# Late tokens of a PEER mixer: indices kept on chip, unwanted rows skipped, the gather ending two units later

## The chip, the cores and the metric

The kernel runs on one core of a Trainium2 chip. The metric is the device time of one execution in microseconds (us). The kernel before the change took 1620.73 us, the median of three timed runs (1619.91 to 1622.59). One more execution was recorded by the hardware profiler; every time below that is not one of those three comes from it.

Engines are called by the names of the profile: PE (matrix multiply; PEld its weight loads), DVE (vector), ACT (activations), POOL (issues the gathers here), SP (issues most plain transfers). Each engine works through its own instructions strictly in order, so an instruction that waits holds up all that stand behind it on the same engine.

## The reference

The input is 512 tokens of width 1024. One layer runs a hybrid mixer (16 state-space heads and 8 attention heads), a layer norm, a PEER expert mixer, and a last layer norm. The change lies in the PEER part, of which the reference reads, cut down:

```python
q = (xb @ w_query).reshape(T, 8, 2, 128)
s = einsum('thkd,hknd->thkn', q, sub_keys)          # 2 x 128 sub-key scores per head
sv, si = top_k(s, 16)                               # best 16 of each half
cand_s = sv[:, :, 0, :, None] + sv[:, :, 1, None, :]
cand_i = si[:, :, 0, :, None] * 128 + si[:, :, 1, None, :]
top_s, top_pos = top_k(cand_s, 16)                  # 16 experts of 16384, per head
expert_idx = take_along_axis(cand_i, top_pos)
gate = softmax(top_s)
u = u_table[expert_idx]                             # 16384 x 1024
act = gelu(einsum('td,thkd->thk', xb, u))
v = v_table[expert_idx]
out = einsum('thk,thkd->td', gate * act, v)
```

So each token picks 8 x 16 = 128 experts. Expert number 128 i + j lies in chunk i of the tables, a chunk being 128 rows.

## The kernel before

**Two ways of doing PEER.** For the first three blocks of 128 tokens the kernel does not gather. It multiplies the tokens with whole chunks: a U chunk (`u_chunk`, 128 rows of the U table against the tokens, then a gelu into `act`), later a V chunk (`v_chunk`, which weighs `act` with a matrix of gates `gt` and multiplies with 128 rows of the V table into the accumulators `va`). There are 128 chunks of each. For the fourth block of tokens the rows are gathered one expert slot at a time: an indirect transfer issued by POOL brings 128 rows of 4 KB, one per token, into a tile `row`, and DVE takes a dot product with the token (U half, line 1830) or adds the row, weighed, to `ac` (V half, line 1850).

**The 32 late tokens.** Of the third block, 32 tokens (`UG`) get their U dots by an early gather. Another 32 tokens, the late ones (`LT`), take part in U chunks 0 to 51 like the rest (`C1` = `LEAD` = 52), but not in chunks 52 to 127, whose products are therefore 320 columns wide and no longer 352. What they need there is gathered late: `late_fetch` (line 1789) issues 32 indirect transfers of 128 rows (32 tokens times 4 experts each), `late_dots` (line 1795) takes 32 dot products on DVE (line 1802), and `late_build` makes gate matrices of them. `late_build` uses only experts in chunks 52 and up, though the rows of all experts are gathered.

**Where the late indices come from.** `ug_index` (line 1192) works out the expert numbers early. SP writes those of the late tokens to a scratch tensor `lgi` in DRAM. At the start of the gather section, some 220 us later, POOL loads them back in the order needed, as tile `lix` (line 1751), and after that loads `lg` and the small identity `lid`.

**How each stage is fed.** Every chunk of U, V and other weights goes through one stream (`Stream`, lines 84 to 138): SP loads a raw chunk of 512 KB into one of three buffers `wir`, ACT rounds it into `wih` or `wihx` (line 114), DVE subtracts to get the remainder `wil` (line 124), and PE multiplies with both parts. A raw buffer is loaded again once DVE has made its remainder.

**Interleaving.** The order of instructions on each engine is written out by the program. The last loop makes one U chunk and one V chunk per turn while U chunks remain, then one V chunk per turn. In each turn it also draws work from the generator `gather()` through `pump`, which emits steps until their estimated cost is used up. Until the 256 row steps of the fourth block begin, that is 4.0 us of estimated cost per turn. From there on the pace is set by:

```python
units = lambda: (128 - uc) * 2 + WV * (uc - vc)
left = units()
want = 271 - max(0.0, 274 * (left - ENDU) / GS[1])   # GS[1] = units() - ENDU at the first row
while more and GS[0] < want:
    more = pump(fill, 0.1)
```

So the rows are to be done when `ENDU` units are left, a unit being half of a U-and-V turn, or, after the last U chunk, 1/0.86 of a V chunk. The pace is fixed at 66 U chunks and 14 V chunks done, when 62 x 2 + 0.86 x 52 = 168.72 units are left.

**Memory at the start of the gather section.** The pool `gs1` holds the staging tile `stg` whose last store to DRAM, `gsp<-stg` (1920 KB, issued by ACT), is still running when the section begins. The pool `gp2` is opened in the place of closed pools. In the built program `stg` lies at bytes 169216 to 185599 of each partition; the tile `x3` with the late tokens (shown as x) begins at 171392 and the first row buffer at 176000, so both must wait for that store. `x3` is loaded by one transfer that reads 32 token rows four times over (outermost size 4, step 0).

Of the kernel before, what the change touches and what calls it, by code (L numbers as in the profile page):

```python
# [11 lines left out]
F32 = mybir.dt.float32  # L12
# [3 lines left out]
I32 = mybir.dt.int32  # L16
U32 = mybir.dt.uint32
AF = mybir.ActivationFunctionType
OP = mybir.AluOpType
# [17 lines left out]
LT = 32  # L37
C1 = LEAD
# [3 lines left out]
ROWS = 5  # L42
STAIRS = ((0, 0, 1, 16), (16, 1, 3, 8), (40, 4, 12, 4))
DOT0, HEAD0 = 1, 36
ENDU = 15
WV = 0.86
GST = (1, 3, 5, 7)
YST = (18, 19, 20, 21, 22, 24, 25, 26)
# [10 lines left out]
def tile_block(ctx: ExitStack, tc: tile.TileContext, I, out):  # L59
    nc = tc.nc  # L60
    ctx.enter_context(tc.manual_schedule())
    V, A, T, G = nc.vector, nc.scalar, nc.tensor, nc.gpsimd
# [18 lines left out]
    def chain(*gs):  # L81
        for g in gs:
            yield from g
# [128 lines left out]
    lgi = dram.tile([LT, 128], I32, name="lgi")  # L212
    lgg, lgh = (dram.tile([LT, 128], F32, name=n) for n in ("lgg", "lgh"))
# [624 lines left out]
    def v_proj(p):  # L838
        wh, wl = item()
        vh = ml.tile([128, NB, 256], F32R, name="vh", bufs=2)  # L840
        vl = ml.tile([128, NB, 256], F32R, name="vl", bufs=2)
        vv[p] = (vh, vl)
        for b2 in range(2):
            ps = pp()
            for e in range(2):
                b = b2 * 2 + e
                bs = slice(b * 128, (b + 1) * 128)
                for k in range(2):
                    ks = slice(k * 256, k * 256 + 256)
                    mm3(ps[:, e * 256:(e + 1) * 256], kvh[:, k, bs], kvl[:, k, bs], wh[:, ks], wl[:, ks],  # L850
                        k == 0, k == 1)
            evac(ps, vh[:, b2 * 2:b2 * 2 + 2].rearrange("p a b -> p (a b)"),
                 vl[:, b2 * 2:b2 * 2 + 2].rearrange("p a b -> p (a b)"))
            yield

    def qk_nope(h):
        wh, wl = item()
        ps = pp()
        for k in range(3):
            ks = slice(k * 128, k * 128 + 128)  # L860
            mm3(ps, wh[:, ks], wl[:, ks], qlh[:, k], qll[:, k], k == 0, k == 2)
        QN[h] = pair("qn")
        A.activation(QN[h][0], ps, AF.Copy, scale=SCALE)
        if h:
            V.scalar_tensor_tensor(QN[h][1], ps, SCALE, QN[h][0], op0=OP.mult, op1=OP.subtract)
        yield
        if h == 0:
            V.scalar_tensor_tensor(QN[h][1], ps, SCALE, QN[h][0], op0=OP.mult, op1=OP.subtract)
        ps = pp()
        for k in range(2):  # L870
            ks = slice(384 + k * 128, 512 + k * 128)
            mm3(ps, wh[:, ks], wl[:, ks], kvh[:, k], kvl[:, k], k == 0, k == 1)
        KN[h] = pair("kn")
        evac(ps, *KN[h])
        yield
# [69 lines left out]
    g = chain(qk_nope(1), v_proj(0))  # L945
# [4 lines left out]
    for st in range(39):  # L950
        h, q = divmod(st, 4)
        if q == 0 and h:
            g = iter(())
            if h < 7:
                g = chain(qk_nope(h + 1), v_proj(h // 2)) if h % 2 == 0 else chain(q_pe(h // 2 + 1), qk_nope(h + 1))
# [234 lines left out]
    GT, UR = {}, {}  # L1190

    def ug_index():
        ijg = IJG[2]
        f = lambda z: z.rearrange("p h k -> p (h k)")
        ix = rt2.tile([128, 128], I32, name="uii")
        V.scalar_tensor_tensor(ix, f(ijg[:, 0]), 128.0, f(ijg[:, 1]), op0=OP.mult, op1=OP.add)
        G.dma_start(ugi, ix[128 - UG:])
        G.dma_start(ugg, f(ijg[128 - UG:, 2]))
        late = slice(128 - UG - LT, 128 - UG)
        nc.sync.dma_start(lgi, ix[late])  # L1200
        nc.sync.dma_start(lgg, f(ijg[late, 2]))
        G.dma_start(UR["ix"], bass.AP(tensor=ugi.tensor, offset=ugi.offset, ap=[[UG, 128 // UG], [128, UG], [1, UG]]))
        G.dma_start(UR["g"], ugg)
        for n in range(3):
            ug_fetch(n)

    def ug_fetch(n):
        if n < UG:
            UR[n] = ug.tile([128, D], F32, name="urow", bufs=3)
            G.indirect_dma_start(out=UR[n], out_offset=None, in_=I["u"],  # L1210
                                 in_offset=bass.IndirectOffsetOnAxis(ap=UR["ix"][:, n:n + 1], axis=0))
# [241 lines left out]
    ijp = pool("ijp", side="right")  # L1453
# [51 lines left out]
    for m in range(17):  # L1505
# [8 lines left out]
        while tm[1] < tm[0] + T_Q:  # L1514
            c = next(fill, None)
            if c is None:
# [7 lines left out]
    G.dma_start(UR["x"], bass.AP(tensor=xsp.tensor, offset=xsp.offset + (3 * 128 - UG) * D,  # L1524
                                       ap=[[0, 128 // UG], [D, UG], [1, D]]))
    UR["ix"] = ijp.tile([128, UG], I32, name="uix")
    UR["g"] = ijp.tile([UG, 128], F32, name="ugw")
    rt2 = pool("rt2")
    lo_on[0] = V
# [112 lines left out]
    LR, LS = {}, [None]  # L1642
# [84 lines left out]
    def gather():  # L1727
        ix = gp_.tile([128, 128], I32, name="ix")
# [5 lines left out]
        LR["gT"] = gp_.tile([128, LT // 2, 2, 2], F16, name="lgT")  # L1734
        l0 = 128 - UG - LT
        jT, _, dT = GT[2]
        A.activation(LR["io"], iotaE, AF.Copy)
        A.activation(LR["d"], dT[:, :, l0:l0 + LT], AF.Copy)
        A.activation(LR["j"], jT[:, l0:l0 + LT], AF.Copy)
# [4 lines left out]
                                ap=[[0, 128 // LT], [D, LT], [1, D]]))  # L1744
        hd = gp2.tile([128, 128], F32, name="hd")
        R = {}
        r3 = pool("r3", side="right")
        IA["t"] = r3.tile([128, 16, 16], F16, name="ia3")
        nc.sync.dma_start(IA["t"].rearrange("p a b -> p (a b)"), I["ch"][:, 256:512])
        lix = r3.tile([128, LT], I32, name="lix")  # L1750
        G.dma_start(lix, bass.AP(tensor=lgi.tensor, offset=lgi.offset, ap=[[LT, 128 // LT], [128, LT], [1, LT]]))
        LR["g"] = r3.tile([LT, 128], F32, name="lg")
        G.dma_start(LR["g"], lgg)
        LR["w"] = r3.tile([LT, 128], F32, name="lw")
        LR["m"] = r3.tile([LT, 2], F32, name="lm")
        LR["id"] = r3.tile([LT, LT], F32, name="lid")
        G.dma_start(LR["id"], I["idn"][:LT, :LT])
        lhd = r3.tile([128, LT], F32, name="lhd")

        def part(h0):  # L1760
# [28 lines left out]
        def late_fetch(n):  # L1789
            if n < LT:  # L1790
                R[n] = gp2.tile([128, D], F32, name="row", bufs=ROWS)
                G.indirect_dma_start(out=R[n], out_offset=None, in_=I["u"],
                                     in_offset=bass.IndirectOffsetOnAxis(ap=lix[:, n:n + 1], axis=0))

        def late_dots():
            for n in range(ROWS - 1):
                late_fetch(n)
            yield 6.0
            for n in range(LT):
                late_fetch(n + ROWS - 1)  # L1800
                r = R.pop(n)
                V.scalar_tensor_tensor(r, r, 1.0, lx, op0=OP.mult, op1=OP.mult, accum_out=lhd[:, n:n + 1])
                yield 1.2
            A.activation(lhd, lhd, AF.Gelu)
            G.dma_start(bass.AP(tensor=lgh.tensor, offset=lgh.offset, ap=[[LT, 128 // LT], [128, LT], [1, LT]]), lhd)
            G.dma_start(LR["w"], lgh)
            LS[0] = late_build()
# [55 lines left out]
    gp_ = pool("gp")  # L1863
# [7 lines left out]
    while vc <= LASTC:  # L1871
# [15 lines left out]
        else:  # L1887
            left = units()
            want = 271 - max(0.0, 274 * (left - ENDU) / GS[1])
            while more and GS[0] < want:  # L1890
                more = pump(fill, 0.1)
            if more and left < ENDU:
                more = pump(fill, 1.2)
# [8 lines left out]
        if GS[0] >= 0 and GS[1] == 0:  # L1902
            GS[1] = units() - ENDU
    held = {}
# [141 lines left out]
```

## Time and profile before

| | |
|---|---|
| median of three timed runs | 1620.73 us |
| profiled execution, its own time | 1615.43 us |
| span of its instructions | 1613.7 us |
| PE busy / DVE busy | 1550.5 us (96%) / 1372.7 us (85%) |
| ACT busy / POOL busy | 682.8 us (42%) / 594.8 us (37%) |
| bytes moved | 421.63 MB, mean 261 GB/s |
| start of the gather section, first late row, first row of the fourth block | about 756, 776.8 and 867.5 us |
| last row of the fourth block added | 1537.3 us |

A row of the timeline gives the start, the duration, engine, line, operation, output and inputs, and in brackets how long the engine had been idle and what ended that. A row of the windows gives, for a stretch of time, the busy time of PE, PEld, DVE, ACT and POOL (with instruction counts), the granted TensorE clock as a share of full speed, the mean busy share of the 16 DMA engines and the rate. A row of the waits gives who waited for whom: total, times, longest.

### The profile page before, as it was taken

How to read it: one execution, taken by the hardware profiler on the slowest of the kernel's cores; microseconds unless marked ns; L12 is line 12 of the kernel's file. 1: busy time of each engine (PE TensorE's matmuls, PEld its weight loads, DVE VectorE, ACT ScalarE, POOL GpSimd, SP SyncE). 2: the span in 40 equal slices, each digit the busy share in tenths (PEclk: the TensorE clock that was granted, in tenths of full speed). 3: DMA queues.
4: the chain of work that ended last, by engine and by line, in shares of the span. 5: the costliest groups of instructions: out<-in, count | busy, mean ns of one | idle time of the engine just before them, and what ended most of it. 6: DMA issues, size and time to landing. Idle time of an engine off the chain costs nothing.

```text
span 1613.7 us, 23969 instructions
## 1 busy us (share of the span) xinstructions
PE 1550.5 (96%) x8726; PEld 1360.9 (84%) x8726; DVE 1372.7 (85%) x2594; ACT 682.8 (42%) x1060; POOL 594.8 (37%) x426
## 2 busy tenths in 40 slices
PE   8999999999999999999699999989999989899998
PEld 6888788888889999999689899888888878788886
DVE  8988678747798999995598998988889888999977
ACT  5574466632334455554234343233333333333332
POOL 0000031300343133300462555665666656666500
PEclk9999999999999999999899999999999999999999
DMA  6242133472433599997898999999999999999972
GB/s 249 93 169 79 50 82 85 147 243 95 123 112 103 183 301 350 351 285 231 297 382 286 320 335 331 339 335 409 354 363 388 379 367 354 385 377 376 376 258 107
DMA packets 163350, 421.63 MB, mean 261 GB/s; under 512 B 14928, under 2 KB 68096, under 8 KB 162976
## 3 DMA queue, kind: packets, MB, share of 16 engines
q1 hardware_dynamic: 61024, 212.37, 37.7%
q0 software_dynamic: 50928, 181.65, 30.4%
q10 hardware_dynamic: 51280, 26.09, 5.4%
q8 instruction: 68, 1.11, 0.3%
q14 instruction: 50, 0.41, 0.1%
HBM read 385.70 MB, written 32.24 MB: 259 GB/s over the span
## 4 chain that ended last, share of the span: by engine, by line
PE 60%; issue 12%; DVE 11%; DMA 9%; POOL 7%; ACT 1%; DVEq 0%; POOLq 0%; SPq 0%; ACTq 0%
POOL row L1819 6%; PE va L1633 6%; PE va L1630 6%; PE va L1629 5%; PE pu L77 5%; PE pu L79 5%; PE pu L78 5%; DMA row<-v,ix 4%; PE pw L77 3%; PE pw L78 3%; PE pw L79 3%; DVE wil L124 3%; PE pa L77 3%; PE pa L79 3%; PE pa L78 3%
## 5 line engine op out<-in xcount | busy, mean ns | idle before, releaser
L114 ACT ACTIVATE wih<-wir 128x1024 fp32r<-128x1024 f32 (+2 forms) x268 | 277.2, 1035 | 389.2 <-DMA wir<-v 163.0
L79 PE MATMUL pu<-XTH,wil 128*128 128x320 f32 (+1 forms) x1000 | 319.4, 319 | 32.6 <-DVE wil L124 32.4
L124 DVE TENSOR_TENSOR wil<-wir,wih 128x1024 fp32r<-128x1024 f32 x236 | 287.6, 1219 | 61.8 <-ACT wih L114 43.9
L77 PE MATMUL pu<-XTH,wih 128*128 128x320 f32 (+1 forms) x896 | 286.7, 320 | 7.7 <-DVE stg L1711 7.3
L1630 PE MATMUL va<-wil,Ph 128*128 128x512 f32 x726 | 284.5, 392 | 0.2 <-DVE wil L124 0.2
L78 PE MATMUL pu<-XTL,wih 128*128 128x320 f32 (+1 forms) x896 | 282.9, 316 | 0.0
L1819 POOL DMA_INDIRECT row<-u,ix x128 | 197.0, 1539 | 139.4 <-DVE row L1830 103.5
L1819 POOL DMA_INDIRECT row<-v,ix x128 | 199.1, 1555 | 115.8 <-DVE ac L1850 92.0
L79 PEld LDWEIGHTS pu<-XTH,wil 128*128 128x128 f32 x1000 | 189.9, 190 | 39.1 <-DVE wil L124 39.0
L77 PEld LDWEIGHTS pu<-XTH,wih 128*128 128x128 f32 x896 | 170.3, 190 | 11.5 <-issue 7.2
L1850 DVE SCALAR_TENSOR_TENSOR ac<-row,hd,ac 128x1024 f32<-128x1024 f32 x128 | 164.2, 1283 | 16.5 <-DMA row<-v,ix 14.3
L1830 DVE SCALAR_TENSOR_TENSOR row<-row,x 128x1024 f32<-128x1024 f32 x128 | 151.8, 1222 | 25.0 <-DMA row<-u,ix 24.9
L78 PEld LDWEIGHTS pu<-XTL,wih 128*128 128x128 f32 x896 | 170.4, 190 | 2.5
L1629 PE MATMUL va<-wih,Ph 128*128 128x512 f32 x432 | 169.4, 392 | 2.9 <-ACT Ph L1604 2.9
L1630 PEld LDWEIGHTS va<-wil,Ph 128*128 128x128 f32 x726 | 136.8, 188 | 26.9 <-DVE wil L124 0.6
L124 POOL TENSOR_TENSOR wil<-wir,wih 128x1024 fp32r<-128x1024 f32 (+3 forms) x32 | 62.7, 1964 | 245.2 <-PE pw L79 114.0
L114 ACT ACTIVATE wihx<-wir 128x1024 fp32r<-128x1024 f32 x67 | 71.0, 1060 | 176.4 <-DMA wir<-v 151.2
L1633 PE MATMUL va<-wih,Pl 128*128 128x512 f32 x432 | 134.5, 393 | 1.1 <-DVE Pl L1612 1.1
L1629 PE MATMUL va<-wihx,Ph 128*128 128x512 f32 x294 | 114.6, 390 | 0.0
L1633 PEld LDWEIGHTS va<-wih,Pl 128*128 128x128 f32 x432 | 81.7, 190 | 19.1 <-DVE Pl L1612 1.9
L1629 PEld LDWEIGHTS va<-wih,Ph 128*128 128x128 f32 x432 | 81.7, 189 | 19.1 <-ACT Ph L1604 3.3
L1633 PE MATMUL va<-wihx,Pl 128*128 128x512 f32 x294 | 90.7, 390 | 0.0
(549 smaller groups left out, 3089.8 us busy)
## 6 DMA issues: line engine op xcount, KB each, us to landing
wir<-ut SPq DMA_DIRECT2D x128, 512.0 KB, 6.5
wir<-v SPq DMA_DIRECT2D x128, 512.0 KB, 6.5
gt<-gsp SPq DMA_DIRECT2D x30, 768.0 KB, 8.8
gsp<-stg ACTq DMA_DIRECT2D x11, 1920.0 KB, 15.4
wir<-wo SPq DMA_DIRECT2D x25, 512.0 KB, 3.7
wir<-wf SPq DMA_DIRECT2D x18, 512.0 KB, 3.7
wir<-wqr SPq DMA_DIRECT2D x16, 512.0 KB, 3.7
de<-acd POOLq DMA_DIRECT2D x8, 512.0 KB, 4.9
```

Source lines behind the costliest of these rows:

```text
L77: T.matmul(ps, lh, rh, start=start, stop=False)
L78: T.matmul(ps, lh, rl, start=False, stop=False)
L79: T.matmul(ps, ll, rh, start=False, stop=stop)
L114: A.activation(h, r, AF.Copy)
L124: self.lo(n).tensor_tensor(l, r, h, op=OP.subtract)
L1629: T.matmul(va[b][e], Ph[b], h[:, cs], start=c == 0, stop=False)
L1630: T.matmul(va[b][e], Ph[b], l[:, cs], start=False, stop=False)
L1633: T.matmul(va[b][e], Pl[b], h[:, cs], start=False, stop=c == (LASTC if b == 2 and e else 127))
L1819: G.indirect_dma_start(out=R[s], out_offset=None, in_=I["u"] if s < 128 else I["v"], in_offset=bass.IndirectOffsetOnAxis(ap=ix[:, s % 128: ...
L1830: V.scalar_tensor_tensor(r, r, 1.0, x3, op0=OP.mult, op1=OP.mult, accum_out=hd[:, s:s + 1])
L1850: V.scalar_tensor_tensor(ac, r, hd[:, s - 128:s - 127], ac, op0=OP.mult, op1=OP.add)
```

## The change

Four things are done.

1. In `ug_index`, DVE makes a second set of indices: to the number of every expert in chunks 0 to 51 it adds 32768, which is past the end of the table. SP stores these to `lgi` and, right behind, loads them back in the order needed into a tile `uli` on chip. At the start of the gather section DVE copies `uli` to `lix`; POOL's load of `lix` is gone.
2. The 32 late indirect transfers get a bound (16383) with which an index beyond it is passed over, so that its row is not brought. The five row buffers are first cleared by DVE, five memsets of 128 x 1024, so that a place whose row is passed over holds a number.
3. POOL's loads of `lg` and `lid` move from ahead of the first late transfers to behind the first four.
4. `ENDU` goes from 15 to 13.

```diff
-ENDU = 15
+ENDU = 13
...
         late = slice(128 - UG - LT, 128 - UG)
-        nc.sync.dma_start(lgi, ix[late])
+        lx_, far = (rt2.tile([128, 128], dt, name=n) for n, dt in (("uil", I32), ("uif", F32)))
+        V.tensor_scalar(far, f(ijg[:, 0]), float(C1), 32768.0, op0=OP.is_lt, op1=OP.mult)
+        V.tensor_tensor(lx_, ix, far, op=OP.add)
+        nc.sync.dma_start(lgi, lx_[late])
         nc.sync.dma_start(lgg, f(ijg[late, 2]))
+        nc.sync.dma_start(UR["li"], bass.AP(tensor=lgi.tensor, offset=lgi.offset, ap=[[LT, 128 // LT], [128, LT], [1, LT]]))
...
     UR["ix"] = ijp.tile([128, UG], I32, name="uix")
+    UR["li"] = ijp.tile([128, LT], I32, name="uli")
...
         jT, _, dT = GT[2]
+        lix = gp_.tile([128, LT], I32, name="lix")
+        V.tensor_copy(lix, UR["li"])
...
-        lix = r3.tile([128, LT], I32, name="lix")
-        G.dma_start(lix, bass.AP(tensor=lgi.tensor, offset=lgi.offset, ap=[[LT, 128 // LT], [128, LT], [1, LT]]))
         LR["g"] = r3.tile([LT, 128], F32, name="lg")
-        G.dma_start(LR["g"], lgg)
         LR["w"] = r3.tile([LT, 128], F32, name="lw")
         LR["m"] = r3.tile([LT, 2], F32, name="lm")
         LR["id"] = r3.tile([LT, LT], F32, name="lid")
-        G.dma_start(LR["id"], I["idn"][:LT, :LT])
...
         def late_fetch(n):
             if n < LT:
                 R[n] = gp2.tile([128, D], F32, name="row", bufs=ROWS)
+                if n < ROWS:
+                    V.memset(R[n], 0.0)
                 G.indirect_dma_start(out=R[n], out_offset=None, in_=I["u"],
-                                     in_offset=bass.IndirectOffsetOnAxis(ap=lix[:, n:n + 1], axis=0))
+                                     in_offset=bass.IndirectOffsetOnAxis(ap=lix[:, n:n + 1], axis=0),
+                                     bounds_check=128 * 128 - 1, oob_is_err=False)
 
         def late_dots():
             for n in range(ROWS - 1):
                 late_fetch(n)
+            G.dma_start(LR["g"], lgg)
+            G.dma_start(LR["id"], I["idn"][:LT, :LT])
             yield 6.0
```

The order on the engines moves at three places. New lines shift the line numbers: 1802 of before is 1810 now, 1612 is 1617, 1586 is 1591, 1792 is 1797, 1850 is 1858, 1856 is 1864.

On DVE at the start of the gather section, before (`wil` is a chunk's remainder, `Pl` and `gt` belong to the gate matrices, `row` is a late dot):

```order
L124 TENSOR_TENSOR wil<-wir,wihx 128x1024
L124 TENSOR_TENSOR wil<-wir,wih 128x1024
L1612 TENSOR_TENSOR Pl<-gt,Ph 128x12x2x32
L124 TENSOR_TENSOR wil<-wir,wih 128x1024
L1802 SCALAR_TENSOR_TENSOR row,lhd<-row,x_8438 128x1024 x2
L124 TENSOR_TENSOR wil<-wir,wih 128x1024
L1586 TENSOR_TENSOR gt<-act,gt 128x11x64
```

and now:

```order
L124 TENSOR_TENSOR wil<-wir,wihx 128x1024
L1743 COPY lix<-uli 128x32
L1796 MEMSET row 128x1024 x4
L124 TENSOR_TENSOR wil<-wir,wih 128x1024
L1617 TENSOR_TENSOR Pl<-gt,Ph 128x12x2x32
L124 TENSOR_TENSOR wil<-wir,wih 128x1024
L1796 MEMSET row 128x1024
L1810 SCALAR_TENSOR_TENSOR row,lhd<-row,x_8446 128x1024 x2
L124 TENSOR_TENSOR wil<-wir,wih 128x1024
L1591 TENSOR_TENSOR gt<-act,gt 128x11x64
```

Four memsets now stand ahead of two remainders and a `Pl`, and a fifth right ahead of the first late dot. The two dots still stand ahead of the third remainder.

On POOL at the same place, before:

```order
L1743 DMA x_8438<-xsp 128x1x1024
L1751 DMA lix<-lgi 128x1x32
L1753 DMA lg<-lgg 32x128
L1757 DMA lid<-idn 32x32
L1792 DMA row<-u,lix 128x1024 x32
```

and now:

```order
L1750 DMA x_8446<-xsp 128x1x1024
L1797 DMA row<-u,lix 128x1024 x4
L1804 DMA lg<-lgg 32x128
L1805 DMA lid<-idn 32x32
L1797 DMA row<-u,lix 128x1024 x28
```

The first four row transfers now follow the load of x at once.

On DVE at the end of the gather, from its last row on, before (`ac` is the fourth block's accumulator; 1856 and lines 167 to 183 are its closing norm):

```order
L1850 SCALAR_TENSOR_TENSOR ac<-row,hd,ac 128x1024
L1586 TENSOR_TENSOR gt<-act,gt 128x10x64
L124 TENSOR_TENSOR wil<-wir,wih 128x1024
L1612 TENSOR_TENSOR Pl<-gt,Ph 128x12x2x32
L124 TENSOR_TENSOR wil<-wir,wihx 128x1024
L1856 SCALAR_TENSOR_TENSOR ac<-x_9375,ac 128x1024
L1586 TENSOR_TENSOR gt<-act,gt 128x10x64
L124 TENSOR_TENSOR wil<-wir,wih 128x1024
L167 BN_STATS lgst<-ac 128x6 x2
```

and now:

```order
L1858 SCALAR_TENSOR_TENSOR ac<-row,hd,ac 128x1024
L1591 TENSOR_TENSOR gt<-act,gt 128x10x64
L124 TENSOR_TENSOR wil<-wir,wih 128x1024
L1617 TENSOR_TENSOR Pl<-gt,Ph 128x12x2x32
L124 TENSOR_TENSOR wil<-wir,wih 128x1024
L1864 SCALAR_TENSOR_TENSOR ac<-x_9450,ac 128x1024
L1591 TENSOR_TENSOR gt<-act,gt 128x10x64
L124 TENSOR_TENSOR wil<-wir,wih 128x1024
L167 BN_STATS lgst<-ac 128x6 x2
```

The pattern is the same, but the whole block stands two V chunks further on in the stream (the second remainder is that of another chunk, `wih` for `wihx`). On SP, the load of `uli` stands between the store of `lgg` and the next load of a U chunk.

## The prediction

> **What bounds the kernel now.** I read the page first: its span, the busy times and the chain's shares.
>
> ```profile
> span 1613.7 us, 23969 instructions
> PE 1550.5 (96%) x8726; PEld 1360.9 (84%) x8726; DVE 1372.7 (85%) x2594; ACT 682.8 (42%) x1060; POOL 594.8 (37%) x426
> PE 60%; issue 12%; DVE 11%; DMA 9%; POOL 7%; ACT 1%; DVEq 0%; POOLq 0%; SPq 0%; ACTq 0%
> ```
>
> PE is the bound nearly everywhere: 63 us of the span are not PE work. So a gain can only come out of those 63 us, and the next view is where they lie, the windows around the gather section and behind it.
>
> ```profile
> 764.00:768.00 4.00, 4.00 (x27) 3.77 (x26) 0.00 (x0) 0.00 (x0) 1.30 (x3) 1.00 0.73 130
> 768.00:772.00 4.00, 4.00 (x22) 3.43 (x21) 0.00 (x0) 0.00 (x0) 0.00 (x0) 1.00 1.02 192
> 772.00:776.00 4.00, 1.28 (x7) 0.87 (x5) 0.00 (x0) 0.00 (x0) 0.00 (x0) 1.00 0.27 89
> 776.00:780.00 4.00, 0.00 (x0) 0.00 (x0) 0.00 (x0) 2.33 (x3) 2.62 (x3) 0.64 0.41 113
> 780.00:784.00 4.00, 0.00 (x0) 0.00 (x0) 1.68 (x3) 0.00 (x0) 3.09 (x4) 0.50 0.93 319
> 784.00:788.00 4.00, 1.98 (x7) 1.98 (x8) 4.00 (x6) 0.85 (x1) 2.18 (x2) 0.50 0.95 342
> 788.00:792.00 4.00, 4.00 (x19) 3.92 (x19) 4.00 (x7) 0.00 (x0) 2.37 (x2) 0.66 0.97 371
> 1000.00:1200.00 200.00, 186.22 (x1041) 165.26 (x1040) 173.75 (x255) 64.36 (x79) 122.49 (x81) 0.98 0.97 363
> 1200.00:1400.00 200.00, 183.31 (x971) 160.29 (x970) 179.44 (x168) 67.42 (x84) 124.11 (x86) 1.00 0.98 371
> 1400.00:1530.00 130.00, 130.00 (x564) 107.36 (x564) 123.88 (x115) 45.86 (x48) 83.71 (x50) 0.98 0.99 377
> ```
>
> Two places matter. PE stands still from 773 to 786, just where the change works, and with the stop the granted clock falls to its lower level. Between 1000 and 1400 PE loses 30.5 us in small pieces while the DMA engines are 97 to 98% busy. From 1400 on PE has no gap. The timelines of PE, DVE, POOL and SP show who is late at 773.
>
> ```profile
> 765.50 0.31 PE L79 MATMUL pu<-XTH,wil 128*128 128x320 f32 x1
> 772.98 0.31 PE L78 MATMUL pu<-XTL,wih 128*128 128x320 f32 x1
> 786.02 0.64 PE L79 MATMUL pu<-XTH,wil 128*128 128x320 f32 x1 [12.74 <-DVE wil L124]
> 757.40 1.23 DVE L124 TENSOR_TENSOR wil<-wir,wih 128x1024 fp32r<-128x1024 f32 x1 [1.90 <-PE va L1630]
> 761.41 1.23 DVE L124 TENSOR_TENSOR wil<-wir,wih 128x1024 fp32r<-128x1024 f32 x1 [1.91 <-ACT wih L114]
> 781.23 1.22 DVE L1802 SCALAR_TENSOR_TENSOR row<-row,x 128x1024 f32<-128x1024 f32 x1 [18.60 <-DMA row<-u,lix]
> 784.76 1.21 DVE L124 TENSOR_TENSOR wil<-wir,wih 128x1024 fp32r<-128x1024 f32 x1
> 762.86 0.70 POOL L1743 DMA_DIRECT2D x<-xsp  x1 [17.80 <-DMA gsp<-stg]
> 763.55 0.70 POOL L1751 DMA_DIRECT2D lix<-lgi  x1
> 776.77 1.00 POOL L1792 DMA_INDIRECT row<-u,lix  x1 [11.47 <-DMA lix<-lgi]
> 778.08 0.98 POOL L1792 DMA_INDIRECT row<-u,lix  x1 [0.31 <-issue]
> 762.35 0.33 SPq L1749 DMA_DIRECT2D ia<-ch  x1
> ```
>
> Read backwards: PE at 786.02 waited for a remainder, which on DVE stood behind two late dots. The first dot kept DVE idle for 18.60 us, waiting for the first late row. POOL could not ask for that row before 776.77, when `lix` had landed. And `lix` was asked for at 763.55, after the store of `stg` had released x and POOL's queue.
>
> **The price of this stop.** PE waits 12.74 us. The granted clock is 0.64 over the four us from 776, so it fell about 2.9 us before 780, near 777.1, and by the same reading of the 0.66 it came back near 790.7. PE worked from 786.0 to 790.7 at half speed, which loses 2.35 us. Together 15.1 us, the most that this place can give back.
>
> **What the change puts there.** The load of `lix` goes; POOL can issue the first row right behind x, at 763.6. But DVE now has memsets to do first, and the first of them must wait for the same store (its buffer lies in `stg`). The end of the store is when SP's L1749, which waits for it too, is issued: 762.35. The trace of before has one memset of this size:
>
> ```profile
> L1844 DVE MEMSET ac<- x1: 912/912/912, 1216.9 to 1216.9; 128x1024 f32 x1
> ```
>
> So four memsets run from 762.4 to 766.0. Behind them wait, in DVE's order, the remainder that was made at 757.40, the `Pl` and the remainder of 761.41. The first of them is used by PE at 765.50 (remainders are used in order; the one at 784.76 is that of 786.02, and counting back chunk by chunk this one belongs to 765.50). It now ends at 766.0 + 1.2 = 767.2: **PE waits 1.7 us**, a wait that was not there. The second remainder ends near 769.3, and PE wants it at 768.96 + 1.7, so it is in time. The fifth memset ends at 770.1. SP's next loads are late too: their raw buffers come free only with these remainders, at about 767 and 769 and no longer at 764.
>
> Then come the two dots. The first needs x and the first row. For x there are three landings in the trace: this load itself, the same pattern for the early tokens (ux), and the plain load of the fourth block at 862, the fast end of the pair:
>
> ```profile
> DMA to landing us min/median/max: 13.3/13.3/13.3
> ux<-xsp POOLq DMA_DIRECT2D x1, 512.0 KB, 10.3
> DMA to landing us min/median/max: 4.9/9.1/13.3
> ```
>
> From 762.86 these give 776.2, 773.2 and 767.8. For the row: from issue at 776.77 to the dot at 781.23 passed 4.5 us, so an issue at 763.6 gives 768.1 when nothing is ahead of it, and x is ahead of it in POOL's queue. I call T the time of the first dot. From the first dot to the end of the remainder took 784.76 + 1.21 - 781.23 = 4.74 us before; PE, 1.7 us late already, wants that remainder at 774.7. So PE waits T + 4.74 - 774.7 us.
>
> - T cannot be before 770.1 (the fifth memset): wait 0.1, the lower bound.
> - T = 774.7, halfway between the 10.3 and the 13.3 of the two loads with this pattern: wait 4.7. I take this. The two raw chunks that ran beside x before come three to five us later now, which speaks for less than 13.3; four row transfers take their place, which speaks against 10.3.
> - T = 776.2 + 4.5 = 780.7, if the first row still takes a whole fetch after x has landed: wait 10.7, the upper bound.
>
> What is special about this load of x stands in the windows: at 772 to 776 only 0.27 of the 16 DMA engines, about four, are still busy, and PE has just run dry. The Trainium skill, "DMA: Bandwidth & Descriptors", section "Rules for kernel authors", says that a leading broadcast of c copies keeps a whole transfer on at most c engines. Here c is 4 and the 0.27 agrees. By that rule alone the load of x is no faster than before whatever else is moved, T is 776.2 and the forecast below would be 1613.
>
> The clock: a wait of 4.7 us against one of 12.7. I charge half of the 2.35 us, with 0 and 2.35 as bounds. Sum for this place: before 15.1, after 1.7 + 4.7 + 1.2 = 7.6, so **a gain of 7.5 us**; bounds 15.1 - 1.8 = 13.3 and 15.1 - 14.7 = 0.4.
>
> **The rows passed over.** If experts are spread evenly, 52 of 128 chunks are 41% of the 32 transfers of 512 KB, some 6.8 MB. What this is worth is read from the stage where they run:
>
> ```profile
> 776.00:845.00 69.00, 58.53 (x313) 53.19 (x314) 57.28 (x79) 22.51 (x28) 44.77 (x32) 0.90 0.96 363
> L1792 POOL DMA_INDIRECT row<-u,lix x32 | 46.0, 1439 | 34.9 <-DVE row L1802 17.4 <-DMA lix<-lgi 11.5 <-issue 5.5
> ```
>
> At 363 GB/s it is 19 us of transfer time, but of the 10.5 us that PE lacks here 10.0 are the stop itself (776 to 786). So the traffic saved buys at most 0.5 us, and I count 0. What the bound adds to an issue on POOL the trace does not show; today 32 of them take 1439 ns each and POOL is idle for 34.9 us ahead of them. I take nothing, as that idle time covers up to about one us more per issue; more than that is a rival below.
>
> **ENDU.** The pace goes from 274/153.72 to 274/155.72 rows per unit. When the last U chunk is done, 0.86 x 52 = 44.7 units are left: want is 218 before and 215 after. So three row steps leave the stretch up to 1400 for the one behind it. Three rows are 1.5 MB, 4 us at the 371 GB/s of the window, in a stretch where PE loses 30.5 us beside a full DMA. Bounds 0 and 4; since not every gap there is a matter of bytes I take **1.5 us of gain**. Behind 1400 PE has no gap with the DMA at 0.99, and takes the three rows.
>
> The end of the gather comes two V chunks later. There the closing norm, then the loads of the last tiles, follow:
>
> ```profile
> 1558.01 1.28 DVE L183 SCALAR_TENSOR_TENSOR ac<-ac,lgy,row 128x1024 f32<-128x1024 f32 x1
> 1561.91 1.56 POOL L1901 DMA_DIRECT2D xr<-xsp  x3
> 1564.38 1.22 DVE L124 TENSOR_TENSOR wil<-wir,wih 128x1024 fp32r<-128x1024 f32 x1 [2.51 <-issue]
> 1585.48 1.04 ACT L1940 ACTIVATE xr<-xr 128x1024 f32<-128x1024 f32 x1
> xr<-xsp POOLq DMA_DIRECT2D x3, 512.0 KB, 14.1
> ```
>
> L183 now stands behind the remainder of 1564.38, so at about 1566.4, 8.4 us later, and the three loads of `xr` end their issue at 1571.9. With 14.1 us they land by 1586.0, where ACT wanted the last at 1585.5. PE does not wait for these, only the final norm does, so I charge 0, with 1 us as the other end. What hid the tail before is nearly used up.
>
> **The early part.** Two DVE operations of 128 x 128 and SP's load of `uli` come in near 539. SP now waits for the landing of `lgi` before the next U chunk.
>
> ```profile
> 538.96 0.37 SPq L1200 DMA_DIRECT2D lgi<-uii  x1
> DMA to landing us min/median/max: 3.4/3.4/3.4
> 542.07 0.35 SPq L96 DMA_DIRECT2D wir<-ut  x1
> 450.00:600.00 150.00, 149.35 (x952) 138.92 (x951) 143.51 (x557) 66.43 (x103) 44.84 (x41) 1.00 0.54 166
> ```
>
> 538.96 + 0.5 + 3.4 + 0.4 = 543.3: the next chunk is asked for 1.2 us later than at 542.07. PE lacks 0.65 us in 150 here; its lead in remainders hides the delay. Without that lead it would cost the 1.2 us. I count 0.
>
> **Sum.** 7.5 + 1.5 = 9.0 us of gain. The profiled execution took 1615.43 us (span 1613.7 and 1.7 around it), 5.3 less than the median of the timed runs; I take the difference over to the median: 1620.7 - 9.0 = 1611.7, so **1612 us**.
>
> **Rivals.**
>
> 1. *Forecast*: the wait for `lix` turns into a shorter wait for x and the memsets. 1612; T between 772.5 and 778 and the ENDU bounds give 1607 to 1616. Chance 0.45.
> 2. *x lands early*, since the two raw chunks are no longer beside it at the start; DVE is then held only by memsets. Gain 13.3 + 1.5: 1606. For it: the plain load took 4.9 us. Against it: ux took 10.3 us, with no raw chunks of V about. Chance 0.25.
> 3. *Nothing comes of it*: rows queue behind x and the first lands a full fetch after it, or the later chunks, asked for at 767 instead of 764, stop PE in their turn. Gain 0.4 + 1.5: 1619. For it: SP's loads do become late, and the chain of waits runs through the gather (POOL, DVE and DMA) behind 870. Chance 0.20, of which half lies within 0.2% of before.
> 4. *Slower: the bounded issue is dear.* The place is POOL's 32 issues. With 46.0 us busy and 34.9 idle, 11.5 of that for `lix`, they span 69.4 us, 2.2 us each, and DVE takes each dot in order ahead of remainders that PE needs. If an issue with its gap came to 3.2 us (its 1.44 nearly doubled, and its gap), 32 x 1.0 = 32 us more, less the idle time left of 17, less 9: 1620.7 + 6 = 1627. It decides from about 2.2 + (17 + 9)/32 = 3.0 us per issue. For it: nothing in the trace has this form. Against it: the same 128 rows with an index each take 1.44 us to issue today, and a comparison per index is little beside that. Chance 0.07.
>
> The skip not passing rows over at all would cost no more than the 0.5 us above, and is no case of its own. The remaining 0.03 goes to a later tail.
>
> **Chances and range.** About 0.2% (3.2 us) is what a measurement of this kernel can tell from no change. Faster by more: 0.45 + 0.25 + half of 0.20 = 0.80. Within: 0.10. Slower: 0.10. The likeliest case has 1607 to 1616 as its own range; taking in rival 2 with the upper end of ENDU's gain and most of rival 3 gives 1603 to 1620.
>
> **What would show it.** Right: the stop at 773 to 786 gone or under 6 us, a new stop of one to three us near 766 behind a memset, the first late row issued near 764 and the first dot near 775, x landing last; the granted clock lower for less than 13.6 us; fewer bytes by some 7 MB; the last row of the fourth block added two V chunks later against PE; no PE gap behind 1400. Wrong: POOL's late issues much above 1.44 us; a wait of DVE for a row after x has long landed; a stop of PE for `wihx` or a remainder near 780 that is as long as the one removed; or `xr` as the last thing waited for in the tail.

## The result and the profile after

The changed kernel takes 1604.42 us (median of four runs, 1603.30 to 1607.92) where the kernel before took 1620.32 beside it (four runs). The ratio is 0.9908, with a 95% interval of 0.9883 to 0.9932: faster, by 15.9 us. Measured twice more beside the kernel before, the ratio was 0.9906 (0.9874 to 0.9939) and 0.9923 (0.9898 to 0.9947), that is 14.1 and 11.4 us; the kernel before stood at 1615.9 and 1613.6 there. The forecast was 1612, a gain of 9.0 us.

The profiled execution of the changed kernel took 1605.51 us, against 1615.43 before. Its page begins:

```profile
span 1603.7 us, 24008 instructions
PE 1548.7 (97%) x8726; PEld 1361.4 (85%) x8726; DVE 1377.9 (86%) x2602; ACT 684.2 (43%) x1060; POOL 590.1 (37%) x425
DMA packets 163450, 414.30 MB, mean 258 GB/s; under 512 B 16823, under 2 KB 69991, under 8 KB 163076
```

PE's time outside its work has gone from 63 to 55 us, and 7.3 MB less are moved. The windows of the changed kernel, at the places that were shown of before (columns: window, length, busy time of PE, PEld, DVE, ACT and POOL with counts, granted clock, DMA share, GB/s):

```profile
764.00:768.00 4.00, 1.62 (x9) 1.15 (x7) 3.68 (x5) 0.00 (x0) 3.39 (x3) 1.00 0.73 135
772.00:776.00 4.00, 3.87 (x18) 3.00 (x16) 0.00 (x0) 0.00 (x0) 1.07 (x1) 1.00 1.04 236
776.00:780.00 4.00, 0.00 (x0) 0.00 (x0) 0.65 (x1) 1.03 (x2) 0.00 (x0) 1.00 0.48 166
780.00:784.00 4.00, 0.48 (x2) 0.48 (x3) 3.49 (x6) 1.40 (x3) 2.43 (x2) 0.61 0.41 132
784.00:788.00 4.00, 4.00 (x17) 4.00 (x17) 4.00 (x7) 1.29 (x2) 1.51 (x2) 0.53 0.91 296
788.00:792.00 4.00, 4.00 (x22) 3.43 (x21) 4.00 (x7) 1.05 (x2) 3.39 (x3) 1.00 0.91 331
776.00:845.00 69.00, 61.48 (x329) 55.91 (x330) 62.69 (x86) 26.41 (x32) 46.03 (x27) 0.95 0.82 282
845.00:1000.00 155.00, 155.00 (x860) 139.75 (x860) 138.26 (x302) 63.82 (x82) 68.94 (x47) 1.00 0.89 310
1400.00:1530.00 130.00, 130.00 (x575) 107.69 (x574) 123.53 (x114) 45.76 (x48) 76.46 (x50) 1.00 0.99 374
```

The stop is still there, shorter, and a small one has come ahead of it at 764 to 768. The clock is at its lower level from 780.9 to 787.7 (0.61 and 0.53 in the windows there), and no longer until 790.7. While the late rows come in (776 to 845) the DMA engines are 82% busy, where they were 96% busy. The timelines of PE, DVE and POOL show what PE waits for now:

```profile
767.98 0.42 PE L79 MATMUL pu<-XTH,wil 128*128 128x320 f32 x1 [2.38 <-DVE wil L124]
783.52 0.64 PE L79 MATMUL pu<-XTH,wil 128*128 128x320 f32 x1 [7.65 <-DVE wil L124]
762.71 0.91 DVE L1796 MEMSET row<- 128x1024 f32 x1 [6.78 <-DMA gsp<-stg]
765.93 0.91 DVE L1796 MEMSET row<- 128x1024 f32 x1 [0.16 <-issue]
766.76 1.16 DVE L124 TENSOR_TENSOR wil<-wir,wih 128x1024 fp32r<-128x1024 f32 x1
779.35 1.22 DVE L1810 SCALAR_TENSOR_TENSOR row<-row,x 128x1024 f32<-128x1024 f32 x1 [8.36 <-DMA row<-u,lix]
762.91 0.70 POOL L1750 DMA_DIRECT2D x<-xsp  x1 [18.02 <-ACT wih L114]
763.92 1.07 POOL L1797 DMA_INDIRECT row<-u,lix  x1 [0.30 <-DVE row L1796]
855.93 0.58 POOL L1819 DMA_DIRECT2D x<-xsp  x1
```

The late rows are asked for at 763.92 instead of 776.77, and yet the first dot comes at 779.35 instead of 781.23: 12.9 us of head start brought 1.9 us. The row landed 15.4 us after its issue, 1.8 us behind x, the load just ahead of it in POOL's queue. That load took longer to land than the 13.3 us of before:

```profile
DMA to landing us min/median/max: 14.6/14.6/14.6
```

**Two measures.** Runs of one kernel spread by 10 us and more (1609.4 to 1626.6 for the kernel before in one comparison), so two measures from the traces stand beside the times. *Late stretch*: from the start of POOL's load of x at the gather's start to the start of its next load of x, that of the fourth block, behind the last late row. Of before that is 762.86 to 862.02, 99.2 us; of the change 762.91 to 855.93, 93.0 us. *PE lost*: in windows of 1 us, PE's idle time plus its busy time times one minus the granted clock, summed from 755 to 1000. Of before 16.1 us, of the change 12.1 us. Only the second is time of the engine that bounds the kernel. PE runs its 8726 matmuls in the same order in every kernel here, so the start of one and the same matmul can be compared: from 755 to 1000 the changed kernel gains 4.2 us on the kernel before, as PE lost says (4.0), and not the 6.2 us of the late stretch, which is time of POOL.

### The profile page after: what moved, and what is told of

It is laid out like the page before. It is cut to its first block, busy times and chain, and to the rows that moved or that the text cites. A ratio compares the mean times of both kernels' runs of the same rounds, so it can differ in the third digit from the quotient of the medians.

```text
span 1603.7 us, 24008 instructions
## 1 busy us (share of the span) xinstructions
PE 1548.7 (97%) x8726; PEld 1361.4 (85%) x8726; DVE 1377.9 (86%) x2602; ACT 684.2 (43%) x1060; POOL 590.1 (37%) x425
## 3 DMA queue, kind: packets, MB, share of 16 engines
q0 software_dynamic: 50896, 174.31, 29.7%
## 4 chain that ended last, share of the span: by engine, by line
PE 65%; issue 10%; DVE 9%; DMA 8%; POOL 6%; ACT 1%; DVEq 0%; POOLq 0%; ACTq 0%
PE va L1638 7%; PE va L1635 7%; PE va L1634 7%; POOL row L1827 6%; PE pu L77 6%; PE pu L79 6%; PE pu L78 6%; DMA row<-v,ix 5%; PE pw L77 3%; PE pw L79 3%; PE pw L78 3%; PE pa L77 3%; PE pa L79 3%; PE pa L78 3%; PE pw L1345 2%
## 5 line engine op out<-in xcount | busy, mean ns | idle before, releaser
L79 PE MATMUL pu<-XTH,wil 128*128 128x320 f32 (+1 forms) x1000 | 319.2, 319 | 27.7 <-DVE wil L124 27.5
L1827 POOL DMA_INDIRECT row<-v,ix x128 | 188.3, 1471 | 130.5 <-DVE ac L1858 104.5
L1858 DVE SCALAR_TENSOR_TENSOR ac<-row,hd,ac 128x1024 f32<-128x1024 f32 x128 | 164.3, 1284 | 15.7 <-DMA row<-v,ix 13.7
L1838 DVE SCALAR_TENSOR_TENSOR row<-row,x 128x1024 f32<-128x1024 f32 x128 | 151.8, 1222 | 18.4 <-DMA row<-u,ix 18.2
```

Of the source, the lines that this page charges most:

```text
L79: T.matmul(ps, ll, rh, start=False, stop=stop)
L1827: G.indirect_dma_start(out=R[s], out_offset=None, in_=I["u"] if s < 128 else I["v"], in_offset=bass.IndirectOffsetOnAxis(ap=ix[:, s % 128: ...
L1838: V.scalar_tensor_tensor(r, r, 1.0, x3, op0=OP.mult, op1=OP.mult, accum_out=hd[:, s:s + 1])
L1858: V.scalar_tensor_tensor(ac, r, hd[:, s - 128:s - 127], ac, op0=OP.mult, op1=OP.add)
```

## The experiments

| kernel | median us (runs) | before, beside it | ratio, 95% | late stretch | PE lost 755 to 1000 | 1000 to 1540 |
|---|---|---|---|---|---|---|
| before | | | | 99.2 | 16.1 | 36.9 |
| changed | 1604.4 (4) | 1620.3 | 0.9908 (0.9883 to 0.9932) | 93.0 | 12.1 | 32.7 |
| after_again | 1601.8 (6) | 1615.9 | 0.9906 (0.9874 to 0.9939) | 93.0 | 12.4 | 31.1 |
| after_third | 1602.2 (6) | 1613.6 | 0.9923 (0.9898 to 0.9947) | 92.6 | 11.6 | 27.5 |
| a_endu15 | 1609.2 (9) | 1615.2 | 0.9960 (0.9939 to 0.9981) | 91.4 | 10.7 | 29.7 |
| b_endu13 | 1608.7 (10) | 1615.2 | 0.9965 (0.9942 to 0.9988) | 100.2 | 16.5 | 31.1 |
| a_noskip | 1608.3 (9) | 1615.2 | 0.9956 (0.9938 to 0.9974) | 98.4 | 14.6 | 26.9 |
| a_noskip2 | 1607.1 (10) | 1613.6 | 0.9951 (0.9923 to 0.9978) | 98.4 | 18.2 | 34.2 |
| a_lateidx | 1608.0 (12) | 1615.2 | 0.9948 (0.9931 to 0.9966) | 95.6 | 12.9 | 31.9 |
| a_lateidx2 | 1604.4 (9) | 1613.6 | 0.9942 (0.9921 to 0.9962) | 96.2 | 14.6 | 34.3 |
| a_x4 | 1597.9 (6) | 1615.9 | 0.9884 (0.9854 to 0.9913) | 88.3 | 7.3 | 27.8 |
| a_poolms | 1604.3 (6) | 1615.9 | 0.9915 (0.9884 to 0.9946) | 91.7 | 11.1 | 34.5 |
| a_x4_poolms | 1598.5 (7) | 1615.9 | 0.9905 (0.9871 to 0.9939) | 89.8 | 9.3 | 24.7 |
| b_x4 | 1610.8 (12) | 1613.6 | 0.9981 (0.9961 to 1.0001) | 95.3 | 12.8 | 29.7 |

The last two columns are PE lost in the two stretches; after_again and after_third are the changed kernel once more. The late stretch repeats within 0.6 us wherever a kernel was profiled more than once, and differs by 1.0 and up to 1.7 us between kernels that differ in ENDU alone, which acts only behind it. PE lost up to 1000 repeats within 0.8 us for the changed kernel and within 3.6 for a_noskip. The last column scatters more (27.5 to 32.7 for the changed kernel).

### ENDU undone, and ENDU alone

```diff
 (a_endu15, in the changed kernel)
-ENDU = 13
+ENDU = 15
 (b_endu13, in the kernel before)
-ENDU = 15
+ENDU = 13
```

> The changed kernel with ENDU back at 15. Theory A (the gain is the shorter stop at the start of the gather section, ENDU gives little): about 1606, 1.5 us above the changed kernel's 1604.4, and the gaps of PE between 1000 and 1400 stay near the 26 us of the changed kernel. Theory B (ENDU relieves the stretch in which the DMA engines are full): 1609 or more, and those gaps come back to about 30 us. Both: the stop at 776 to 784 as in the changed kernel, 10 us in two pieces.

> The kernel before with ENDU 13 as its only change. Theory A: 1618 to 1620, at most 2 us below before. Theory B: 1615 to 1616, and the gaps of PE between 1000 and 1400 fall from 30.5 to about 26 us with the stop of 12.7 us at 773 unchanged.

Each stands about 6 us below the kernel before, which was itself at 1615.2 beside them and not at the 1620 that the expectations start from. b_endu13 leaves the stop as it was; the waits of PE between 740 and 1000 in its trace (total, times, longest):

```profile
PE pu L79 <- DVE wil L124: 14.0, 4, 12.2
```

So ENDU alone is worth 6.4 us (1.9 to 9.4 by the interval of the ratio), though it changes nothing at the gather's start, and the rest of the change without ENDU is worth 6.0. Theory B was nearer in time. Its sign in the gaps came in one kernel only: PE's idle time between 1000 and 1400 was 23.6 us in b_endu13, but 24.7 and not about 30 in a_endu15.

Which waits ENDU shortens the profiles don't show. PE lost 31.1 us between 1000 and 1540 in b_endu13 against 36.9 before; but the two other kernels with ENDU 15 stand at 29.7. A single execution varies too much there, and the profiled ones of these two were the fastest of their kernel (1602.4 and 1606.2, 7 and 5 us below the median). The table as a whole still bears ENDU out. Subtract from each kernel's gain in time what its PE loses less than that of before up to 1000. With ENDU 15 (a_endu15, b_x4), 0.6 and -0.5 us are left; with ENDU 13, 4.0 to 11.9 us, in all eleven rows.

### Every row brought

```diff
-V.tensor_scalar(far, f(ijg[:, 0]), float(C1), 32768.0, op0=OP.is_lt, op1=OP.mult)
+V.tensor_scalar(far, f(ijg[:, 0]), 0.0, 32768.0, op0=OP.is_lt, op1=OP.mult)
```

The bounded transfers and the clears stay, but no index is moved past the end.

> The changed kernel with the threshold for passing rows over at 0, so that every late row is brought; memsets, bound and the rest stay. Theory A: no change, 1604 to 1605, since PE has no gap while the late rows run except the stop itself. Rival C (the rows passed over are what lets x, the raw chunks and the first rows land): 1608 or more, first dot at 782 or later instead of 779.4. Both: 7 MB more moved.

> The changed kernel with every row of the gather brought over, as in the first call, where it stood 7.2 us below the kernel before. My reckoning (rows that are passed over are worth nothing: first dot at 780.0 against 779.4, TensorE's waits 10.0 us either way): within 2.5 us of the changed kernel beside it, so 11 to 15 us below the kernel before. Rival (the 7.3 MB less to bring do count): 5 to 8 us above the changed kernel, as the first call and the second seem to say together.

The first comparison alone didn't settle it, since the changed kernel was not part of it. Beside the changed kernel (after_third), the one that brings every row is 4.9 us slower, outside the 2.5 us that I expected by then; the two intervals overlap. The traces are clearer. The late stretch is 98.4 us both times, nearly that of before, and PE loses 14.6 and 18.2 us, on either side of the 16.1 of before. Two windows of a_noskip, to be held against those of the changed kernel, with PE's two waits:

```profile
776.00:845.00 69.00, 62.52 (x331) 56.66 (x330) 58.64 (x81) 22.62 (x28) 41.41 (x27) 0.93 0.95 363
845.00:1000.00 155.00, 153.92 (x845) 138.46 (x844) 142.25 (x305) 65.46 (x86) 66.33 (x48) 1.00 0.90 313
763.82 0.70 POOL L1750 DMA_DIRECT2D x<-xsp  x1 [17.99 <-ACT wih L114]
862.26 0.58 POOL L1819 DMA_DIRECT2D x<-xsp  x1
768.88 0.41 PE L79 MATMUL pu<-XTH,wil 128*128 128x320 f32 x1 [2.42 <-DVE wil L124]
784.77 0.63 PE L79 MATMUL pu<-XTH,wil 128*128 128x320 f32 x1 [6.47 <-DVE wil L124]
```

The repeat, a_noskip2, behind 845, and the kernel before there:

```profile
845.00:1000.00 155.00, 152.22 (x828) 137.24 (x827) 139.43 (x303) 63.91 (x83) 63.96 (x47) 0.99 0.88 308
845.00:1000.00 155.00, 154.38 (x850) 139.16 (x849) 143.68 (x309) 64.70 (x84) 70.64 (x49) 1.00 0.90 317
```

The DMA engines are as full as before (0.95, 363 GB/s), the granted clock is lower over the stretch (0.93 against 0.95), DVE gets less done (58.64 against 62.69 us), and behind 845 PE has gaps again (1.1 and 2.8 us), where the changed kernel has none. So passing over rows is worth 5.6 us of the late stretch (98.4 against 92.9, the mean of three) and 4.4 us of PE's losses (16.4, the mean of two that lie 3.6 apart, against 12.0). The stop is not where it lies: the two waits make 8.9 and 10.6 us with every row brought, and 8.0 to 10.0 in the changed kernel. The rival's sign, a first dot at 782 or later, did not come either (779.99 and 780.17). PE loses 4.6 and 4.8 us to the lower clock, against 1.7 to 4.4, and the rest is the gaps behind 845. With every row brought, all else that was done at the gather's start (early indices, clears, the later loads of `lg` and `lid`) brings 0.8 us of the stretch, no more than the stretch scatters.

### Indices late again

```diff
-        V.tensor_copy(lix, UR["li"])
...
+        G.dma_start(lix, bass.AP(tensor=lgi.tensor, offset=lgi.offset, ap=[[LT, 128 // LT], [128, LT], [1, LT]]))
```

The load stands behind that of x, as before; rows are still passed over.

> The changed kernel with the late indices loaded by POOL behind x again, at the start of the gather section. Theory A (the wait for the indices is what was removed): first late row issued only at about 777.5, when the indices have landed, first dot at 782, one stop of about 10 us near 774 to 784 beside that of 2.4 us, 1607 to 1608, 3 us above the changed kernel. Rival D (x, not the indices, sets the first dot, and the rows land with x anyway): first dot at 779 to 780, 1604 to 1605.

> The changed kernel with the late indices loaded behind x again. My reckoning (x, not the indices, sets the first dot: 779.23 here against 779.35): within 2.5 us of the changed kernel beside it, so 11 to 15 us below the kernel before. Rival (the early indices bring the gain of the gather's start): 5 to 8 us above the changed kernel.

Timeline of POOL and DVE in a_lateidx, and the landing of x:

```profile
763.75 0.71 POOL L1749 DMA_DIRECT2D x<-xsp  x1 [18.00 <-ACT wih L114]
775.25 1.08 POOL L1797 DMA_INDIRECT row<-u,lix  x1 [10.09 <-DMA lix<-lgi]
779.23 1.28 DVE L1810 SCALAR_TENSOR_TENSOR row<-row,x 128x1024 f32<-128x1024 f32 x1 [7.39 <-DMA row<-u,lix]
DMA to landing us min/median/max: 10.6/10.6/10.6
```

The rows are asked for 11.3 us later than in the changed kernel, and the first dot comes at the same time. Without row transfers beside it, x lands in 10.6 us (11.6 in the repeat). In the repeat x was asked for 1.6 us later, `lix` landed 11.3 us behind its issue and not 10.0, and the first dot stood at 782.12. The late stretch is 95.9 us on the mean, 3.0 longer than with early indices, and PE loses 1.7 us more (13.8, the mean of two, against 12.0). The time beside the changed kernel is 2.2 us longer: within the 2.5 that I expected, and the intervals don't separate it from nothing. So the traces give early indices 2 to 3 us once rows are passed over, less than the rival's 5 to 8; the times neither confirm nor exclude it.

### The changed kernel again, and x as the cause

```diff
-        G.dma_start(lx, bass.AP(tensor=xsp.tensor, offset=..., ap=[[0, 128 // LT], [D, LT], [1, D]]))
+        for e in range(128 // LT):
+            G.dma_start(lx[e * LT:(e + 1) * LT], bass.AP(tensor=xsp.tensor, offset=..., ap=[[D, LT], [1, D]]))
 (a_poolms and a_x4_poolms)
-                    V.memset(R[n], 0.0)
+                    G.memset(R[n], 0.0)
```

> The changed kernel as it is, beside the three below. In the runs before, its indices alone (ENDU 15) stood 6.0 us below the kernel before, and ENDU 13 alone 6.4 us. Theory A2 (the two gains lie in different stretches, 760-1000 and 1000-1400, and add up): 1602 to 1604 where the kernel before stands at 1615, that is 11 to 13 us below it. Rival B2 (either edit frees the same slack, the weight loads' lead over TensorE, and the second adds nothing): 6 to 7.5 us below it, as the four runs before all were. In the profile both expect TensorE's two waits at the start of the gather again, 2.4 and 7 to 8 us, or one of them smaller where the weight loads have run ahead.

> The late x by four plain loads of 32 rows instead of one load that repeats 32 rows four times; nothing else. Theory X (the repeated load sits on four DMA engines for 14.6 us and the first gathered rows stand behind it there): its landing falls from 14.6 us to 8 or less, the first dot comes at 771 to 775 instead of 779.35, TensorE's second wait falls from 7.65 us to 0 to 3, and the time is 3 to 7 us below the changed kernel run beside it. Rival R (the gathered rows are themselves what is slow, at the about 0.35 us that a packet of 4 KB takes there): x lands earlier, but the first dot stays at 778 to 780 and the time within 2 us. Three more issues on GpSimd, 0.70 us each, put the first row's issue 2.1 us later under either.

> The five clears of row buffers on GpSimd instead of VectorE; the loads as in the changed kernel. My reckoning: VectorE forms the first remainder at 762.7 to 764 instead of 766.76, so TensorE's first wait (2.38 us, wil) goes; SyncE issues its weight loads at 764 again instead of 768; the five clears cost GpSimd 1 to 4 us each, so the rows are issued 3 to 10 us later. Theory X (x and the rows behind it set the first dot): the first dot moves by less than the rows' issue does, and the time is 1 to 3 us below the changed kernel. Rival R: the first dot moves by as much as the rows' issue, to 783 or later, TensorE's second wait grows from 7.65 to 10 or more, and the time is the same or up to 4 us above it.

> Both edits together: x by four plain loads, and the clears on GpSimd. Theory X: the first wait of TensorE (2.38 us) goes and the second stands at 0 to 4 us, since the first dot is set by the rows' issue on GpSimd (five clears and three more loads ahead of it) at 773 to 779; 4 to 8 us below the changed kernel. Rival R: the first dot is at 783 or later, and the time is no lower than the changed kernel's.

after_again is 14.1 us below the kernel before (9.9 to 20.4 by its interval), so the two gains of about 6 us add up, and rival B2, which had 6 to 7.5 us, falls.

a_x4, timelines of POOL, DVE and PE, and the landings of its four loads:

```profile
763.67 1.95 POOL L1751 DMA_DIRECT2D x<-xsp  x4 [18.28 <-ACT wih L114]
765.92 1.07 POOL L1798 DMA_INDIRECT row<-u,lix  x1 [0.30 <-issue]
851.97 0.57 POOL L1820 DMA_DIRECT2D x<-xsp  x1
771.67 1.16 DVE L1811 SCALAR_TENSOR_TENSOR row<-row,x 128x1024 f32<-128x1024 f32 x1
768.74 0.42 PE L79 MATMUL pu<-XTH,wil 128*128 128x320 f32 x1 [2.64 <-DVE wil L124]
787.23 0.41 PE L79 MATMUL pu<-XTH,wil 128*128 128x320 f32 x1 [2.98 <-DVE wil L124]
DMA to landing us min/median/max: 2.9/3.4/3.6
```

Theory X holds. The same 512 KB as four loads land within 3.6 us of each issue, and within 5.1 us of the first, and not after 14.6. (The edit drops the repeat and splits the load at once; the two were not tried apart.) The first dot no longer waits for anything but the fifth clear (771.67), the stop of 7.65 us is gone, and a smaller one of 2.98 us has come behind the fifth and sixth dots, which wait 2.25 and 1.41 us for their rows. The late stretch falls by 4.7 us and so does what PE loses. In time it is 3.9 us below the changed kernel beside it, within the 3 to 7 expected, but the intervals overlap. Its median is the lowest of all; it is faster than the kernel before.

a_poolms takes the 2.38 us wait away and gives it back:

```profile
764.26 0.97 POOL L1796 MEMSET row<- 128x1024 f32 x1
782.09 0.64 PE L79 MATMUL pu<-XTH,wil 128*128 128x320 f32 x1 [8.28 <-DVE wil L124]
```

The first dot stands at 778.52, behind x (12.9 us) and the row that follows it, and PE, no longer held up earlier, waits longer there. The first dot behaved as theory X has it (the rows are asked for 1.6 us later, at 765.51, and the dot comes 0.8 us earlier), but the 1 to 3 us of time did not come: the time is the same within what can be measured (1604.3 against 1601.8). With both edits two waits of 2.86 and 3.15 us are left, and the time is that of a_x4, 3.4 us below the changed kernel and not 4 to 8.

### x alone, in the kernel before

> The changed kernel once more, now beside its two one-part versions below, since those were compared with the kernel before in another call than the changed kernel was. All theories expect 12 to 16 us below the kernel before, as in the call before this one (1601.8 against 1615.9).

> The kernel before with one edit: the late x by four plain loads of 32 rows. No indices kept, no rows passed over, no clears, ENDU 15. Theory X (the indices were late because they were brought on the same queue behind a repeated load that took 13.3 us): the indices land 4 to 8 us after their issue instead of 13.0, the first late row is issued at 770 to 774 instead of 776.8, the first dot comes at 774 to 778 instead of 781.2, TensorE's stop falls from 12.7 us to 4 to 9, and the time is 4 to 9 us below the kernel before. Rival (the indices' own load is slow, 4096 elements of 128 B pieces and smaller): they still land 12 us after their issue, the stop stays at 11 us or more, and the time is within 2 us of the kernel before.

The edit is that of a_x4, in the kernel before. POOL, DVE and PE, and the landing of `lix`:

```profile
765.18 0.72 POOL L1752 DMA_DIRECT2D lix<-lgi  x1
771.92 0.99 POOL L1793 DMA_INDIRECT row<-u,lix  x1 [5.03 <-DMA lix<-lgi]
776.44 1.23 DVE L1803 SCALAR_TENSOR_TENSOR row<-row,x 128x1024 f32<-128x1024 f32 x1 [13.77 <-DMA row<-u,lix]
780.87 0.64 PE L79 MATMUL pu<-XTH,wil 128*128 128x320 f32 x1 [7.51 <-DVE wil L124]
DMA to landing us min/median/max: 6.5/6.5/6.5
```

The indices land 6.5 us after their issue, where they took 13.0 us behind the repeated load:

```profile
DMA to landing us min/median/max: 13.0/13.0/13.0
```

Row, dot and stop come where theory X put them, and the late stretch is 3.9 us shorter. The time is 2.8 us below the kernel before, less than the 4 to 9 that I expected and just within what the runs cannot tell from no change (the interval reaches 1.0001). So half of what made `lix` late was the repeated load of x; the other 6.5 us remain without it.

## Why the prediction was right or wrong

The direction, the range and the place of the stop were right. The forecast time was 7.6 us too high; by gains, 9.0 us were forecast and 11.4 to 15.9 measured. The terms were further off than the sum: the place of the stop gave less than forecast, ENDU more. That these two errors have opposite signs is luck.

- **The bound: PE, and the stop at 773 to 786.** Right: from 755 to 1000 PE loses 4.0 us less.
- **The memsets, 1.7 us.** Right in kind, and 2.38 us in size: between two of them lie 0.16 us, and the first began at 762.71 and not at 762.35. SP's loads came at 767.99 and 769.95, about 1 us later than reckoned, and stopped nothing.
- **T = 774.7, halfway between two landings of x.** This step failed. T was 779.35, near the upper bound of 780.7. I named the four row transfers as what speaks against a quick landing, and gave them too little weight: with them x took 14.2 to 14.6 us in the three profiles of the changed kernel, more than either landing I had, and 12.9 to 13.9 in four of its variants; without them, in a_lateidx and its repeat, 10.6 and 11.6. PE's wait there was 7.65 us and not 4.7. At the gather's start this came nearest to rival 3 (rows queue behind x), to which I gave 0.20.
- **The sentence on the skill.** The Trainium skill, "DMA: Bandwidth & Descriptors", section "Rules for kernel authors", says that a leading broadcast of c copies confines a transfer to at most c engines. The traces agree: x landed at 777.5, no sooner than the 776.2 put beside that sentence, and four loads without the broadcast took at most 3.6 us each where the one took 14.6.
- **The clock, 1.2 us.** It was at its lower level for 6.8 us instead of 13.7 (10.2 and 6.8 in the repeats), but PE worked through more of it: it lost 2.1 us to it (4.4 and 1.7), against 2.4 before and the 1.2 charged. In all the place cost 12.1 us where I had 7.6, a gain of 4.0 (3.7 and 4.5 in the repeats) against the 7.5 forecast.
- **The rows passed over, "at most 0.5 us".** This step failed too. I took PE's stop out of the sum first and asked what traffic costs the rest. The stop did stay, but with all rows brought the clock is low for longer and PE has gaps behind 845, outside the stretch that I looked at; the rest of the change then gives nearly nothing there (a stretch of 98.4 us against 99.2). The skip is worth 4.4 us of PE's losses, and 4.9 us in a time that the intervals do not separate.
- **The bounded issue, 0.** Right, and rival 4 was far off. The issues take 1518 and 1539 ns with every row brought and 1658 ns in the changed kernel, against 1439. The 7.0 us more that they take stand beside 10.9 us less of POOL's idle time, 24.0 us now against 34.9:

```profile
L1797 POOL DMA_INDIRECT row<-u,lix x32 | 53.0, 1658 | 24.0 <-DVE row L1810 18.5 <-DVE wil L124 3.7 <-issue 1.2
```

- **ENDU, 1.5 us, bounds 0 to 4.** Mis-sized: 6.4 us in time (1.9 to 9.4). I valued three rows by their transfer time (4 us) and bounded the gain by it. Which waits give the rest stays open.
- **The tail and the early part, 0.** Right: PE's lead over the kernel before is 0.1 us at 755, and the same at 1450 as at the end (9.8). The last row was added 67.2 us ahead of the end (76.4 before), two chunks later as reckoned; `xr` landed in 11.8 us, and PE has no gap from 1400 to 1530. The chunk behind `uli` was asked for at 543.24, reckoned 543.3.
- **Rival 2 (1606)** has nearly the time that came out, but not its reason: x landed later, not early.

By time the parts add up: 6.4 us for ENDU alone and 6.0 for the rest make 12.4, where the three comparisons of the whole gave 11.4 to 15.9. PE lost up to 1000 accounts for 3.7 to 5.4 of those 6.0. Moving the loads of `lg` and `lid` was not tried alone.

## What to carry to other kernels

An early request brings little where its answer queues behind a slow transfer: ask what stands ahead of it on the same DMA engines, and what the earlier requests will do to that transfer. A stop of the bounding engine does not show all that the traffic beside it costs: here the bytes saved left the stop as long as it was and shortened the time at the lower clock and the gaps that came behind it. When a change has several parts, price each one alone and together with the others: here two parts that were priced at 7.5 and 1.5 us came to about 6 us each. And measure a gain on the engine that bounds the kernel: POOL's stretch became 6.2 us shorter where PE gained 4.2.

## What the runs showed of the hardware that was not expected

- A load of 512 KB that repeats 32 rows four times landed in 10.6 to 14.6 us, by what ran beside it; as four loads of 128 KB each landed within 3.6 us (5.4 in a_x4_poolms, 5.6 in b_x4), at 1.25 us more issue time on POOL (1.95 against 0.70).
- An indirect issue that passes rows over takes POOL no less time: 1658 ns on the mean (1552 to 1698 in the nine profiles that pass rows over), against 1518 and 1539 ns with every row brought, though 32 issues move 7.3 MB less. Part of it may be other waits inside the issue; that was not tried apart.
- Clearing a buffer of 128 x 1024 takes 0.97 us on POOL and 0.91 us on DVE.
